# Adaptive average pooling: partition p owns block p/8 + 16 (p mod 8) of the rows in place of block p

## The chip, the cores and the metric

The kernel runs on one core of one Trainium2 chip. The metric is the time of one execution on the device in microseconds (us); lower is better. Before the change the median of three runs is 333.54 us (333.31 to 333.57).

## The reference

The input x has 32 batches of 256 channels of 4096 float32 values. The output has 256 values for each batch and channel: value i is the mean of the 16 neighbouring inputs from 16 i to 16 i + 15.

```
for i in range(output_size):
    start = int(i * length / output_size)
    end = int((i + 1) * length / output_size)
    result[:, :, i] = np.mean(x[:, :, start:end], axis=-1)
```

Batches and channels are alike for this, so the kernel sees 8192 independent rows of 4096 values (16 KiB) that become rows of 256 values (1 KiB). The input is 134.2 MB, the output 8.4 MB.

## The kernel before

The 8192 rows are worked through in 16 tiles of 512 rows: 128 partitions by R = 4 rows. The first 15 tiles come from the first 7680 rows. They are cut into 128 blocks of 60 neighbouring rows (960 KiB of input, 60 KiB of output), and partition p owns block p. In tile t each partition loads rows 4t to 4t+3 of its block, one contiguous run of 64 KiB, so that a load is 128 runs (8.4 MB). The sixteenth tile takes the last 512 rows, four neighbouring rows to a partition (x_last, o_last).

The pattern of a load has two sides. On the DRAM side x_many (line 46) is [partition][60 x 4096 values], from which line 69 cuts the 16384 values of tile t. On the SBUF side the tile xin is [128 partitions][16384 values].

In the loop (lines 62 to 88) each tile goes through the same steps:
- Line 70: SP issues the load of the tile into xin. The pool inpool (line 53) has two buffers, so the load of tile t+2 waits until the work on tile t is done.
- Line 73: POOL (GpSimd) takes the second half of the tile's 1024 windows and adds their upper 8 values to their lower 8, in place.
- Line 78: DVE (VectorE) sums the 16 values of each window of the first half, at the same time.
- Line 81: DVE sums the 8 values that POOL left of each window of the second half.
- Line 84: ACT (ScalarE) multiplies the 1024 sums by 1/16, in place.

The results of the 15 tiles stay in SBUF in res_many, 60 KiB for each partition, and leave in one store of 7.86 MB into o_many (line 47, issued by line 72 through store, line 58). SP issues it after the load of the last tile, once the ACT of tile 14 is done. The results of the last tile (res_last) leave in two stores at the end (line 90): 120 partitions, then the other 8.

All transfers are issued by SP, on one queue, in program order. Tile's scheduler places the waits of loads and compute; the three stores are counted on a semaphore of their own (line 60), on which SP waits at the end (line 95).

Of the kernel before, what the change touches and what calls it, by code (L numbers as in the profile page):

```python
# [1 line left out]

# [4 lines left out]


@with_exitstack
def kernel(  # L10
    ctx: ExitStack,
    tc: tile.TileContext,
    x: bass.AP,
    output_size: int,
    out: bass.AP,
):

    nc = tc.nc
    F32 = mybir.dt.float32
    X = mybir.AxisListType.X

    batch, channels, length = x.shape
    ob, oc, olen = out.shape
    assert ob == batch and oc == channels and olen == output_size
    assert length % output_size == 0
    window = length // output_size  # L30
    hw = window // 2
    inv_w = 1.0 / float(window)

    P = nc.NUM_PARTITIONS
    R = 4
    rows = batch * channels
    assert rows % (P * R) == 0
    ntiles = rows // (P * R)
    many = (ntiles - 1) * R
    cells = R * output_size  # L40
    m = cells // 2
    cols = R * length

    xr = x.rearrange("b c l -> (b c) l")
    orow = out.rearrange("b c o -> (b c) o")
    x_many = xr[0 : P * many, :].rearrange("(p r) l -> p (r l)", p=P, r=many)
    o_many = orow[0 : P * many, :].rearrange("(p r) o -> p (r o)", p=P, r=many)
    x_last = xr[P * many :, :].rearrange("(p r) l -> p (r l)", p=P, r=R)
    o_last = orow[P * many :, :].rearrange("(p r) o -> p (r o)", p=P, r=R)

    res_many = nc.alloc_sbuf_tensor("res_many", [P, (ntiles - 1) * cells], F32, align_bytes=256)
    res_last = nc.alloc_sbuf_tensor("res_last", [P, cells], F32, align_bytes=256)
    inpool = ctx.enter_context(tc.tile_pool(name="inpool", bufs=2))

    stored = nc.alloc_semaphore("stored")

    def store(out, in_):
        ins = nc.sync.dma_start(out=out, in_=in_)
        tc.no_tile_sem_insts.add(ins.ins.name)
        ins.then_inc(stored, 16)  # L60

    for t in range(ntiles):
        last = t == ntiles - 1
        xin = inpool.tile([P, cells, window], F32, name="xin")
        if last:
            res, base, src = res_last, 0, x_last
        else:
            res, base = res_many, t * cells
            src = x_many[:, t * cols : (t + 1) * cols]
        nc.sync.dma_start(out=xin.rearrange("p o w -> p (o w)"), in_=src)  # L70
        if last:
            store(o_many, res_many[:, :])
        nc.gpsimd.tensor_add(  # L73
            out=xin[:, m:cells, 0:hw],
            in0=xin[:, m:cells, 0:hw],
            in1=xin[:, m:cells, hw:window],
        )
        nc.vector.reduce_sum(  # L78
            out=res[:, base : base + m], in_=xin[:, 0:m, :], axis=X
        )  # L80
        nc.vector.reduce_sum(  # L81
            out=res[:, base + m : base + cells], in_=xin[:, m:cells, 0:hw], axis=X
        )
        nc.scalar.mul(  # L84
            out=res[:, base : base + cells],
            in_=res[:, base : base + cells],
            mul=inv_w,
        )
    for lo, hi in ((0, 120), (120, P)):
        store(o_last[lo:hi, :], res_last[lo:hi, :])  # L90

    ctx.pop_all().close()
    tc.close()
    tc.compile()  # L94
    nc.sync.wait_ge(stored, 48)
    nc.sync.sem_clear(stored)


# [1 line left out]
_INS = ['x', 'output_size']  # L100
_OUTS = [((32, 256, 256), 'float32')]

_NUMBERS = {'output_size': 256}


# [26 lines left out]
```

## Time and profile before

| what | us |
|---|---|
| median of 3 runs | 333.54 (333.31 to 333.57) |
| the profiled execution, its own time | 333.37 |
| its span, from the first instruction to the last | 332.1 |
| first load lands (first reduction starts) | 22.72 |
| last load lands (last L78 starts) | 312.86 |
| large store issued | 307.67 |
| two small stores issued | 327.26 |
| L78 on DVE, one instruction | 8.69 |
| L73 on POOL, one instruction | 8.72 |
| L81 on DVE, one instruction | 4.42 |
| L84 on ACT, one instruction | 1.06 |
| median from a load's issue to its landing | 25.3 |

The page gives for each engine its busy time and its share of the span. DMA engines are no such engine: the core's 16 DMA engines are shown together, by the packets of each queue (number, MB, and the time that the packets took as a share of 16 engines' span), and by rows of 40 slices with the mean busy share in tenths and the GB/s moved. The bytes of a packet are counted where it starts, so that slices shorter than a packet jump up and down. There is one clock value for TensorE, which this kernel doesn't use. A load's time to landing includes the time that it stands behind the load ahead of it in the queue.

### The profile page before, as it was taken

The page shows a single profiled execution, that of the slowest core. Times are in us where ns is not written, and L with a number is a line of the kernel's source. Part 1 is how long each engine was busy: PE and PEld are TensorE (multiplying, and loading weights), DVE is VectorE, ACT ScalarE, POOL GpSimd, SP SyncE. Part 2 cuts the span into 40 slices and gives each one's busy share as a digit, 9 for nine tenths or more (in the row PEclk, how much of TensorE's full clock was granted, in tenths as well). Part 3 has the DMA queues.
Part 4 walks back from the last instruction along what each step waited for, and adds up shares of the span by engine and source line. Part 5 has one row for each costly group of instructions (what it writes and reads, how often), then busy time and mean ns, then how long its engine had stood idle before and what let it go on. Part 6 is the DMA issues. An engine that isn't in the chain of part 4 may idle for free.

```text
span 332.1 us, 160 instructions
## 1 busy us (share of the span) xinstructions
DVE 209.7 (63%) x32; ACT 18.2 (5%) x17; POOL 139.7 (42%) x20
## 2 busy tenths in 40 slices
DVE  0029396692939669293966939295693929569392
ACT  1000101001010100101010010101000010100001
POOL 0027091542709164270916427090643709063270
DMA  9898999989899998989899998989999898989997
GB/s 379 379 505 379 474 411 426 458 379 505 379 489 395 450 434 379 505 379 505 379 474 411 395 489 379 505 379 489 395 450 434 379 505 379 505 379 474 395 466 307
DMA packets 2599, 142.61 MB, mean 429 GB/s; under 512 B 295, under 2 KB 295, under 8 KB 423
## 3 DMA queue, kind: packets, MB, share of 16 engines
q1 hardware_dynamic: 2599, 142.61, 99.4%
HBM read 134.22 MB, written 8.39 MB: 429 GB/s over the span
## 4 chain that ended last, share of the span: by engine, by line
DMA 66%; POOL 18%; DVE 11%; POOLq 3%; issue 0%; ACT 0%; SPq 0%
DMA xin<-in_x_dram 66%; POOL xin L73 18%; DVE res_many L81 9%; POOLq L94 3%; DVE res_last L81 1%; ACT res_last L84 0%; SPq L70 0%; POOLq L73 0%
## 5 line engine op out<-in xcount | busy, mean ns | idle before, releaser
L73 POOL TENSOR_TENSOR xin<-xin 128x4096 f32<-128x4096 f32 x16 | 139.5, 8719 | 181.7 <-DMA xin<-in_x_dram 181.7
L78 DVE TENSOR_REDUCE res_many<-xin 128x512 f32<-128x8192 f32 x15 | 130.3, 8686 | 107.4 <-DMA xin<-in_x_dram 107.4
L81 DVE TENSOR_REDUCE res_many<-xin 128x512 f32<-128x4096 f32 x15 | 66.3, 4420 | 2.5 <-POOL xin L73 2.3
L84 ACT ACTIVATE res_many<-res_many 128x1024 f32<-128x1024 f32 x15 | 15.9, 1057 | 289.8 <-DVE res_many L81 289.8
L78 DVE TENSOR_REDUCE res_last<-xin 128x512 f32<-128x8192 f32 x1 | 8.7, 8686 | 6.3 <-DMA xin<-in_x_dram 6.3
L81 DVE TENSOR_REDUCE res_last<-xin 128x512 f32<-128x4096 f32 x1 | 4.4, 4420 | 0.2 <-POOL xin L73 0.2
L84 ACT ACTIVATE res_last<-res_last 128x1024 f32<-128x1024 f32 x1 | 1.1, 1057 | 18.5 <-DVE res_last L81 18.5
L84 ACT ACT_TABLE_LOAD x1 | 1.3, 1283 | 0.7 <-PEq L113 0.7
L113 POOL MEMSET const-float32-0.0<- 128x1 f32 x1 | 0.1, 99 | 0.2 <-issue 0.2
L113 POOL MEMSET const-bfloat16-1.0<- 128x1 bf16 x1 | 0.1, 103 | 0.0
L113 POOL MEMSET const-uint8-127<- 128x1 uint8 x1 | 0.1, 103 | 0.0
L113 POOL MEMSET const-float32-1.0<- 128x1 f32 x1 | 0.1, 99 | 0.0
## 6 DMA issues: line engine op xcount, KB each, us to landing
out_dram<-res_many SPq DMA_DIRECT2D x1, 7680.0 KB
out_dram<-res_last SPq DMA_DIRECT2D x1, 480.0 KB
xin<-in_x_dram SPq DMA_DIRECT2D x16, 25.3
out_dram<-res_last SPq DMA_DIRECT2D x1, 32.0 KB
```

The costliest lines, as they stand in the source:

```text
L73: nc.gpsimd.tensor_add(out=xin[:, m:cells, 0:hw], in0=xin[:, m:cells, 0:hw], in1=xin[:, m:cells, hw:window],)
L78: nc.vector.reduce_sum(out=res[:, base : base + m], in_=xin[:, 0:m, :], axis=X)
L81: nc.vector.reduce_sum(out=res[:, base + m : base + cells], in_=xin[:, m:cells, 0:hw], axis=X)
L84: nc.scalar.mul(out=res[:, base : base + cells], in_=res[:, base : base + cells], mul=inv_w,)
L94: tc.compile()
L113: nc = _bacc.Bacc("TRN2", target_bir_lowering=False, num_devices=1)
```

## The change

The 128 blocks of 60 rows are given to the partitions in another order. The DRAM sides of the 15 loads and of the large store get a dimension more: 16 (a) by 8 (b), where partition 8a + b owns block 16b + a. Partition 0 owns block 0, partition 1 block 16, partition 7 block 112, partition 8 block 1, and so on. Partitions that follow each other within a group of eight are 16 blocks (15 MiB of input) apart in DRAM; partitions that are eight apart own neighbouring blocks. The SBUF sides are as before, as are the last tile, all compute instructions and the order of issue. Load and store use the same order, so each result goes to its own row.

```diff
     xr = x.rearrange("b c l -> (b c) l")
     orow = out.rearrange("b c o -> (b c) o")
-    x_many = xr[0 : P * many, :].rearrange("(p r) l -> p (r l)", p=P, r=many)
-    o_many = orow[0 : P * many, :].rearrange("(p r) o -> p (r o)", p=P, r=many)
+    A = 16
+    B = P // A
+    x_many = xr[0 : P * many, :].rearrange("(b a r) l -> a b (r l)", a=A, b=B, r=many)
+    o_many = orow[0 : P * many, :].rearrange("(b a r) o -> a b (r o)", a=A, b=B, r=many)
     x_last = xr[P * many :, :].rearrange("(p r) l -> p (r l)", p=P, r=R)
     o_last = orow[P * many :, :].rearrange("(p r) o -> p (r o)", p=P, r=R)
...
             res, base = res_many, t * cells
-            src = x_many[:, t * cols : (t + 1) * cols]
+            src = x_many[:, :, t * cols : (t + 1) * cols]
         nc.sync.dma_start(out=xin.rearrange("p o w -> p (o w)"), in_=src)
         if last:
             store(o_many, res_many[:, :])
```

## The prediction

> **What bounds the kernel now.** I read the sum of the page first (busy time by engine, then the DMA queue), then the chain that ended last, then a table of stretches that I cut where the first packets start (1.73, from the 40 slices of the first 3 us) and where reductions start, then the timeline around one issue. The page says which resource is full:
>
> ```profile
> DVE 209.7 (63%) x32; ACT 18.2 (5%) x17; POOL 139.7 (42%) x20
> ...
> q1 hardware_dynamic: 2599, 142.61, 99.4%
> HBM read 134.22 MB, written 8.39 MB: 429 GB/s over the span
> ...
> DMA 66%; POOL 18%; DVE 11%; POOLq 3%; issue 0%; ACT 0%; SPq 0%
> ```
>
> No engine is busy for more than 63% of the span, while the packets of the one DMA queue fill 99.4% of what 16 DMA engines have. The chain names POOL and DVE too (18% and 11%), but that is the buffer's turn: a load is issued when its buffer is free and then queues behind the load before it. The table of stretches says what a load costs in the steady state (columns: stretch, its length, busy time of DVE, ACT and POOL, granted clock, share of the 16 DMA engines, GB/s):
>
> ```profile
> 1.73:22.72 20.99, 0.00 (x1) 0.29 (x1) 0.00 (x0) 1.00 1.07 450
> ...
> 80.74:273.96 193.22, 131.06 (x20) 10.57 (x10) 87.19 (x10) 1.00 1.00 434
> ...
> 293.27:312.86 19.59, 13.11 (x2) 1.06 (x1) 8.72 (x1) 1.00 0.99 425
> ```
>
> A packet counts where it starts, which gives the first stretch a share above 1: it holds starts of the second load. The middle row spans ten loads: 193.22 / 10 = 19.32 us a load, at a DMA share of 1.00. Per load DVE works 13.1 us and POOL 8.7 us; both then wait. A load moves 128 x 64 KiB = 8.39 MB, and 8.39 MB / 19.32 us is the 434 GB/s of the row, 27.1 GB/s for each of 16 engines. The timeline shows how far ahead of need a load is issued:
>
> ```profile
> 94.05 0.33 SPq L70 DMA_DIRECT2D xin<-in_x_dram  x1
> 94.05 1.06 ACT L84 ACTIVATE res_many<-res_many 128x1024 f32<-128x1024 f32 x1 [18.33 <-DVE res_many L81]
> 100.07 8.69 DVE L78 TENSOR_REDUCE res_many<-xin 128x512 f32<-128x8192 f32 x1 [6.05 <-DMA xin<-in_x_dram]
> ```
>
> The load is issued at 94.05, the one ahead of it lands at 100.07: 6.0 us of spare time for the issue. So time moves only if the rate of the 16 DMA engines moves, or the first load's start, or the tail.
>
> **The change, part by part.** No instruction is added or removed. The same 15 loads (L70) and the one large store (L58, 7.86 MB) keep their bytes, their number of contiguous runs (128 runs of 64 KiB a load, 128 of 60 KiB in the store) and their SBUF side. Two things differ, both on the DRAM side.
>
> *Which rows a partition reads.* The blocks stay 60 rows = 960 KiB apart, in another order. The trace shows 434 GB/s with one order and no other. Below: nothing, the runs are as long as before. Above: no row shows a load slowed by DRAM placement, and the nearest one is the first load, 20.99 us in place of 19.32, which carries the cold start. If every one of the 14 other changed loads ran like that it would be 14 x 1.67 = 23.4 us. I take 0: the steady rows are flat at 434 to 435 GB/s over addresses that move on with every load.
>
> *The shape of the DRAM side.* It was [128][run], it is [16][8][run], while the SBUF side stays [128][run]. If the 16 DMA engines share a transfer by its outermost dimension, then each now gets one of the 16 outer entries, and so eight neighbouring partitions (8a to 8a+7), in that order. Which engine serves which partition isn't in the trace. If the old split gave each engine a way into SBUF of its own, and the new one lets two engines meet on one way while another way stands empty, a load takes up to twice its time.
>
> Bounds for one load: nothing is gained below, since the share is already 1.00; above, 2 x 19.32 = 38.64 us, +19.32. For the 15 changed loads: 0 to 15 x 19.32 = +289.8 us. The sixteenth load (x_last) keeps its shape. For the large store: at 434 GB/s it takes 7.86 / 434 = 18.1 us, so 0 to +18.1.
>
> Which end? For the direction out of SBUF there is a near row. The tail's 480 KB store has 120 partitions, which 16 doesn't divide, so it can't have the split of a 128-partition transfer. It fills most of the last microsecond of traffic:
>
> ```profile
> DMA  7839977339997079999087994843994000000000
> GB/s 328 328 164 655 655 328 328 164 164 819 492 492 328 0 328 655 492 492 492 0 328 328 655 655 164 328 164 164 492 656 164 0 0 0 0 0 0 0 0 0
> DMA packets 95, 0.30 MB, mean 295 GB/s; under 512 B 23, under 2 KB 23, under 8 KB 95
> ```
>
> This is the stretch 330.7 to 331.7, in 40 slices. Traffic fills 31 of them: 295 x 40 / 31 = 381 GB/s with packets of 4 KiB, no sign of a halving (217). So I put the large store at +0 and keep +18.1 for the range. For the direction into SBUF no row shows any split but the old one; the rows are at 434, the two ends are 0 and +289.8. I take the upper end, and that is a choice: the present rate is exactly flat at full share, which is how 16 separate ways look, and the change pairs engines up with nothing in it that sets them apart.
>
> [...]
>
> *Issue.* A three-dimensional pattern may cost SP more than the 0.33 us of a load's issue. The 6.0 us between issue and the landing of the load ahead hide that; with loads twice as long the spare time is longer still. Without that cover each extra microsecond would cost 15.
>
> *Waits and the compute engines.* The change adds no wait. DVE and POOL work on the same tiles; they wait 19 us longer per load if the loads double. Nothing queues behind that except the ACT scaling and the next issue, which has the whole of the longer load ahead of it. The tail is as before: last load, 13.2 us of POOL and DVE beside the large store, ACT, two small stores.
>
> **The sum.** The profiled execution: span 332.1, time 333.37, so 1.3 us lie around the span, and the median of the runs shown, 333.54, is 0.17 above it. 333.37 + 289.8 (15 loads) + 0 (store) = 623.2. [...] The 16 first packets start from 1.73 to 2.85, within about a microsecond of each other, by the same 40 slices; with 0.1 us for the pair that is closest together, 15 x 0.2 = 3 us come off. With the 0.17: 620.
>
> **Rivals.**
> *A, two engines meet all the way (forecast).* 620; 600 with a lead of 0.8 us (15 x 1.6 = 24 off), 641 with no lead and a doubled store. For it: a share of exactly 1.00 and a regrouping that pairs engines. Against it: the 120-partition store. If only 8 engines took part the loads would double as well, and the DMA share of the loads would show 0.5.
> *B, the pairs draw apart.* If one engine of a pair gets more of the shared way, its lead grows, and a lead of half a load (9.66 us) ends the meeting. [...] Anything from 340 to 600. A DRAM order that is dearer (up to +23.4) falls into its lower end, 334.2 to 357.
> *C, nothing meets (the other side: not slower).* The ways into SBUF have room for two engines, as the ways out seem to have in the 120-partition store. Then the share of 1.00 is the engines' own limit, every load stays at 19.32 us, and the time is 333.5. It decides if the loads still run at 434 GB/s.
> *D, faster.* C, and the new order also takes away the cold start of the first load (20.99 - 19.32 = 1.7 us) and the slower last one (19.59 - 19.32 = 0.3 us): at most 2.0 us, 331.5 to 332.8. The rest is bytes at full share, so nothing larger can be gained.
>
> **How the numbers follow.** A 0.54, B 0.27 (0.04 of it below 345), C 0.14, D 0.05. The time is A's, 620. The range reaches from 345 to 645: all of A and B but its lowest part, 0.77, about what is asked; going on to C would take in 0.95 and a stretch in which little lies. A measurement of this kernel tells about 0.2% from no change. Faster by over 0.2%: D, 0.05. Within: C, 0.14. Slower: A and B, 0.81.
>
> **What the changed kernel's profile would show.** Under A: the starts of L78's reductions 38 us apart in place of 19.32, stretches of loads near 220 GB/s with a packet share that stays near 1.00 (packets last longer, all 16 engines hold one), the same 2599 packets, DVE near 34% of the span, and the last load (the unchanged shape) back at about 19.6 us. The large store back at 18 us puts the doubling on the way in alone; 36 us puts it on both. Under B the distance between reductions shrinks from load to load. Under C the page is the same to the tenth. A packet count other than 2599 would mean that runs were cut, and my price for the shape would be wrong from the start; so would loads that double with a share of 0.5.

## The result, and the profile after

The changed kernel takes 669.53 us (median of three runs, 668.88 to 669.72) against 333.54 us before: 2.007 times as long, 95% interval 2.004 to 2.009. The direction was as forecast, the time lies 24.5 us above the upper end of the range (645). The profiled execution took 668.88 us with a span of 667.6. Where runs of one kernel further down lie more than 1.5% apart (pairs_apart_2, pitch_64_rows), the faster ones are the ones to compare.

The page of the changed kernel, the same lines as before the change (the lines of the code are two further down now: L72 is the load, L75 POOL, L80 and L83 DVE, L86 ACT, L60 the stores):

```profile
DVE 209.7 (31%) x32; ACT 18.2 (3%) x17; POOL 139.7 (21%) x20
...
q1 hardware_dynamic: 2599, 142.61, 99.7%
HBM read 134.22 MB, written 8.39 MB: 214 GB/s over the span
```

The engines are busy for the same 209.7, 18.2 and 139.7 us. The queue has the same 2599 packets and the same 142.61 MB, and its share of the 16 DMA engines is 99.7%, as full as before. Yet the rate is 214 GB/s in place of 429. A full share says only that every DMA engine holds a packet at all times, not that the packets move at full speed: by their records the median packet of 64 KiB takes 5.12 us in place of 2.42.

The table of stretches of the changed kernel, cut at the starts of the reductions (stretch, length, busy time of DVE, ACT and POOL, granted clock, DMA share, GB/s):

```profile
84.43:570.56 486.13, 157.27 (x25) 12.67 (x12) 104.61 (x12) 1.00 1.00 207
611.30:630.37 19.07, 13.11 (x3) 1.06 (x1) 8.72 (x1) 1.00 1.01 436
630.37:667.60 37.23, 13.10 (x2) 1.06 (x1) 8.72 (x1) 1.00 0.92 199
```

The first row is twelve loads of the new shape: 486.13 / 12 = 40.51 us a load in place of 19.32, at 207 GB/s. The second row is the last load, which kept its shape: 19.07 us, 436 GB/s, on the same queue with the 16 engines just as full (share 1.01). The third row is the tail with the large store: 37.23 us, where the kernel before had

```profile
312.86:332.06 19.20, 13.11 (x2) 1.06 (x1) 8.72 (x1) 1.00 0.89 386
```

The difference of the two spans, 667.6 - 332.1 = 335.5, closes over these pieces. The last reduction of the 15 changed tiles starts at 611.30 in place of 293.27, +318.0 (15 x 21.2). The last load gives back 19.59 - 19.07 = 0.5, and the tail costs 37.23 - 19.20 = +18.0.

The issue of a load costs SP more with the three-dimensional pattern, 0.54 us in place of 0.33 in the steady state, and lies under 27 us of spare time, as these two lines of the changed kernel's timeline show:

```profile
178.77 0.54 SPq L72 DMA_DIRECT2D xin<-in_x_dram  x1
...
205.97 8.69 DVE L80 TENSOR_REDUCE res_many<-xin 128x512 f32<-128x8192 f32 x1 [27.23 <-DMA xin<-in_x_dram]
```

### The profile page after: what moved, and what is told of

It is laid out like the page before. It is cut to its first block, busy times and chain, and to the rows that moved or that the text cites. A ratio compares the mean times of both kernels' runs of the same rounds, so it can differ in the third digit from the quotient of the medians.

```text
span 667.6 us, 160 instructions
## 1 busy us (share of the span) xinstructions
DVE 209.7 (31%) x32; ACT 18.2 (3%) x17; POOL 139.7 (21%) x20
## 2 busy tenths in 40 slices
DMA packets 2599, 142.61 MB, mean 214 GB/s; under 512 B 295, under 2 KB 295, under 8 KB 423
## 3 DMA queue, kind: packets, MB, share of 16 engines
q1 hardware_dynamic: 2599, 142.61, 99.7%
## 4 chain that ended last, share of the span: by engine, by line
another core or an unknown queue 62%; POOL 18%; DMA 13%; POOLq 1%; DVE 1%; issue 0%; ACT 0%
POOL xin L75 18%; DMA xin<-in_x_dram 13%; POOLq L96 1%; DVE res_last L83 1%; DVE res_many L83 1%; ACT res_last L86 0%; POOLq L75 0%
## 5 line engine op out<-in xcount | busy, mean ns | idle before, releaser
L80 DVE TENSOR_REDUCE res_many<-xin 128x512 f32<-128x8192 f32 x15 | 130.3, 8686 | 425.5 <-DMA xin<-in_x_dram 425.5
L75 POOL TENSOR_TENSOR xin<-xin 128x4096 f32<-128x4096 f32 x16 | 139.5, 8718 | 499.3 <-DMA xin<-in_x_dram 499.3
L83 DVE TENSOR_REDUCE res_many<-xin 128x512 f32<-128x4096 f32 x15 | 66.3, 4420 | 2.5 <-POOL xin L75 2.3
L86 ACT ACTIVATE res_many<-res_many 128x1024 f32<-128x1024 f32 x15 | 15.8, 1056 | 607.8 <-DVE res_many L83 607.8
L80 DVE TENSOR_REDUCE res_last<-xin 128x512 f32<-128x8192 f32 x1 | 8.7, 8686 | 5.8 <-DMA xin<-in_x_dram 5.8
L83 DVE TENSOR_REDUCE res_last<-xin 128x512 f32<-128x4096 f32 x1 | 4.4, 4420 | 0.2 <-POOL xin L75 0.2
L86 ACT ACTIVATE res_last<-res_last 128x1024 f32<-128x1024 f32 x1 | 1.1, 1056 | 18.0 <-DVE res_last L83 18.0
```

The costliest lines, as they stand in the source:

```text
L75: nc.gpsimd.tensor_add(out=xin[:, m:cells, 0:hw], in0=xin[:, m:cells, 0:hw], in1=xin[:, m:cells, hw:window],)
L80: nc.vector.reduce_sum(out=res[:, base : base + m], in_=xin[:, 0:m, :], axis=X)
L83: nc.vector.reduce_sum(out=res[:, base + m : base + cells], in_=xin[:, m:cells, 0:hw], axis=X)
L86: nc.scalar.mul(out=res[:, base : base + cells], in_=res[:, base : base + cells], mul=inv_w,)
```

## The experiments

Theory 1 is that of the forecast: the shape of the DRAM side. It supposes that with an outer dimension of 16 each DMA engine gets eight neighbouring partitions, and that two engines are then always on the same way into or out of SBUF; no trace shows which engine serves which partition. Theory 2, the rival, is the order of the blocks in DRAM: engines that read adjacent blocks, or blocks 15 MiB apart, are slow together. The change made both edits at once. Beside each group of runs the kernel before was timed again; its medians are 333.33 to 333.58 us, and the ratios below are to these.

### The shape without the order, and the order with it: loads_old_order, loads_only

The first keeps the neighbourhood of the old order. The 4 rows between groups are there so that the two dimensions can't be merged into one.

```diff
-    x_many = xr[0 : P * many, :].rearrange("(b a r) l -> a b (r l)", a=A, b=B, r=many)
+    x_many = xr[0 : A * 484, :].rearrange("(a s) l -> a s l", a=A, s=484)[:, 0 : B * many, :]
+    x_many = x_many.rearrange("a (b r) l -> a b (r l)", b=B, r=many)
-    o_many = orow[0 : P * many, :].rearrange("(b a r) o -> a b (r o)", a=A, b=B, r=many)
+    o_many = orow[0 : P * many, :].rearrange("(p r) o -> p (r o)", p=P, r=many)
```

> The 15 loads keep the [16][8] shape, but partition 8a + b reads a block that lies next to its old one (block 8a + b, moved on by 4a rows so that the two dimensions don't merge into one); the large store has its old shape and old places. Left out and changed: results of blocks a > 0 are those of rows 4a further on. Theory 1, the shape (each engine gets eight neighbouring partitions, and two engines meet on one way into SBUF): the loads stay at 40.5 us as in the changed kernel, 15 x 21.2 = 318 over the kernel before, so about 651 us. Theory 2, the order of the blocks in DRAM: the old order is back, 19.32 us a load, about 333.5 us.

Measured: 651.04 us (ratio 1.952, 1.946 to 1.958). The second run has the last edit alone, the store's:

> Changed kernel, but the large store has its old one-dimensional shape and places. Changed: the results of a partition go to the place of block p. Both theories: the loads at 40.5 us, the store back from 36.4 to 18.1 us, 669.5 - 18.3 = 651 us. What it tells apart is whether the store's share of the loss is its own (651) or the tail of the loads (669).

Measured: 651.33 us (ratio 1.953, 1.947 to 1.958). The two agree to 0.3 us although their loads read in quite different orders. The stretch of twelve loads, first in loads_old_order (84.99 to 570.92), then in loads_only (84.55 to 570.20):

```profile
84.99:570.92 485.93, 157.27 (x25) 12.67 (x12) 104.61 (x12) 1.00 1.00 207
```

```profile
84.55:570.20 485.65, 157.28 (x25) 12.67 (x12) 104.60 (x12) 1.00 1.00 207
```

40.49 and 40.47 us a load. The shape alone carries the whole loss of the loads; the new order of the blocks costs nothing that these runs can tell. That two engines meet on SBUF's side is not yet shown by this: it only shows that where in DRAM they read makes no difference here.

### The store alone: store_only, store_old_order

store_only has the old x_many and the new o_many.

> Kernel before, but the large store has the new shape and order. Changed: results go to other places. If the ways out of SBUF are shared in the same manner as the ways in, the store takes 36.4 us in place of 18.1: 333.5 + 18.3 = 352 us. If the store was slow in the changed kernel only because it follows the loads, 333.5 us.

Measured: 351.06 us (ratio 1.053, 1.050 to 1.056), +17.5 us. store_old_order adds the same trick with 4 rows between groups on the store's side:

> store_only with the [16][8] shape, but in the old neighbourhood: partition 8a + b stores to the place of block 8a + b moved on by 4a rows (of the last tile's rows 64 are not stored, 16 partitions). Theory 1, the shape: 351 us as in store_only. Theory 2, the order of the places in DRAM makes the store slow: 333.5 us.

Measured: 352.10 us (ratio 1.056, 1.053 to 1.059). So the store's doubling is its own and the shape's too. By the records of its 128 packets of 60 KiB, the median one took 4.72 us in store_only and 2.27 us in the kernel before.

### How many engines, how many ways: eight_engines

```diff
-    A = 16
+    A = 8
```

> Changed kernel with the outer dimension 8 and the inner 16 (partition 16a + b owns block 8b + a) for loads and large store. [...] Theory 1 with meetings between two engines: 8 engines with 16 packets each, each packet 5.07 us as in the changed kernel, 81.1 us a load: 2.2 + 15 x 81.1 + 19.8 + 16 x 4.79 + 1.5 = about 1317 us, DMA share about 0.5. If nothing met and only the number of engines counted: packets of 2.418 us, 38.7 us a load, 2.2 + 15 x 38.7 + 19.8 + 16 x 2.267 + 1.5 = about 640 us, share 0.5. If the outer dimension doesn't set the engines: 669 us, share 1.0.

Measured: 1296.44 us (ratio 3.887, 3.835 to 3.938). The page of this kernel:

```profile
DMA packets 2471, 142.61 MB, mean 109 GB/s; under 512 B 167, under 2 KB 167, under 8 KB 295
## 3 DMA queue, kind: packets, MB, share of 16 engines
q1 hardware_dynamic: 2471, 142.61, 51.4%
```

A share of 51.4% in place of 99.7%: with the outer dimension of 8, half of the engines' time holds no packet. There are 128 packets fewer than the 2599 of the changed kernel, all among those under 512 B (167 in place of 295), eight for each of the 16 changed transfers. Both fit eight engines in place of 16. And in the time that holds a packet the data move at half speed as well: 107 GB/s at a share of 0.50 over the stretch of four loads, 13.4 GB/s for each of eight engines in place of 27.1,

```profile
163.98:482.11 318.13, 52.43 (x9) 4.22 (x4) 34.87 (x4) 1.00 0.50 107
```

79.5 us a load, a quarter of the old rate. Were the number of engines all that counts, it would be 38.7 us and 640 us in all. One factor of two is in the share; the other fits engines that meet, as theory 1 expected with about 1317 us, but this run shows neither that they meet nor on what.

### Setting the pairs apart: two_rows, two_rows_pairs_apart, two_rows_pairs_together

Which engines meet, if any do, is in no trace; that it is engines e and e + 4 is an assumption of these runs. If those two meet because they walk through the same ways in step, a head start of half a load for one of them should end it, although the shape stays as it is. For this the tiles are halved, so that four loads can be under way.

```diff
-    R = 4
+    R = 2
-    inpool = ctx.enter_context(tc.tile_pool(name="inpool", bufs=2))
+    inpool = ctx.enter_context(tc.tile_pool(name="inpool", bufs=4))
```

> Changed kernel with tiles of 2 rows a partition (runs of 32 KiB) and 4 buffers: 31 loads of the new shape and one of the old. It is the control for the two runs with a head start. Theory 1: a load takes half of 40.5 us, 31 x 20.25 us, and the total stays near 669 us, since engines that meet still meet all the way.

Measured: 671.38 us (ratio 2.014, 2.006 to 2.021). The two runs with small loads ahead, which assume that a transfer on n partitions goes to the first n engines, add, with 12 and 4 partitions or with 8,

```diff
+    for n, first in ((12, 0), (12, 1), (12, 2), (12, 3), (4, 4), (4, 5), (4, 6), (4, 7)):
+        nc.sync.dma_start(
+            out=res_many[first : first + 9 * (n - 1) + 1 : 9, 0:cols],
+            in_=xr[0 : n * R, :].rearrange("(p r) l -> p (r l)", p=n, r=R),
+        )
```

> As two_rows, with 8 small loads of 32 KiB a partition ahead of the first (into res_many, which is written over later): four on 12 partitions and four on 4 partitions. If a transfer on n partitions is dealt to the first n engines, engines 0 to 3 get 8 packets, 4 to 11 get 4, 12 to 15 get none, so that each engine e is four packets, half a load, apart from engine e + 4. Theory 1 with pairs e and e + 4 on one way: the meetings end and stay ended, a load takes about 9.7 to 11 us, the store partly doubled: 333.5 + 10 (small loads) + 5 to 45 = 350 to 390 us. Theory 2 (DRAM order) or other pairs: no gain, 669 + 10 = about 680 us.

> As two_rows, with 8 small loads on 8 partitions each, the same 64 packets of 32 KiB in all: engines 0 to 7 start 8 packets behind engines 8 to 15, and the engines e and e + 4 stay level. Theory 1 with pairs e and e + 4: no gain, 669 + 10 = about 680 us. If any unevenness of the engines ended the meetings: near 350 to 400 us, as in two_rows_pairs_apart.

Measured: 670.10 us (ratio 2.010, 2.006 to 2.014) and 687.90 us (ratio 2.063, 2.053 to 2.073). Neither came near 350 to 390: this experiment failed to show what it was made for. The timeline of SP in two_rows_pairs_apart shows that the head start was small (start, duration, issue):

```profile
0.73 5.79 SPq L60 DMA_DIRECT2D res_many<-in_x_dram  x8
6.57 3.98 SPq L78 DMA_DIRECT2D xin<-in_x_dram  x4
```

Eight small loads hold SP for 5.79 us, and the first large load is issued at 6.57. Four packets of 1.21 us (their length at full speed, by the records) can be over by then, so by the assumed deal engines 4 to 11 may have had no delay left and only engines 0 to 3 started late. The records don't show even these apart: of the 3888 packets of 32 KiB that start between 12 and 600 us, none takes less than 2.16 us. So either the lead was lost at once, or engines that meet slow the others too. This run can't tell which.

### The same with longer small loads: pairs_apart_2, pairs_together_2

In place of the eight small loads of 32 KiB a partition:

```diff
+    w = 15360
+    for n, first in ((12, 0), (12, 1), (12, 2), (12, 3), (4, 4), (4, 5)):
+        nc.sync.dma_start(
+            out=res_many[first : first + 9 * (n - 1) + 1 : 9, 0:w],
+            in_=xr[0 : n * 4, :].rearrange("(p r) l -> p (r l)", p=n, r=4)[:, 0:w],
+        )
```

> [...] Here the small loads are fewer and longer: four of 60 KiB on 12 partitions, two on 4 partitions, so that both groups of pairs start about 4.5 us apart (half a load is 4.84). Theory 1 with pairs e and e + 4: loads of 9.7 to 11 us, 333.5 + 14 (the last engines' start) + up to 30 = 345 to 380 us. If the pairs are others, or no lead lasts: 671 + 14 = about 685 us.

> Control for pairs_apart_2: seven small loads of 60 KiB on 8 partitions, the same 56 packets, so that engines 0 to 7 start 16 us behind engines 8 to 15 and e and e + 4 stay level. Theory 1 with pairs e and e + 4: no gain, 671 + 16 = about 687 us. If any unevenness among the engines ended the meetings: near pairs_apart_2.

Measured: pairs_apart_2 takes 444.37 and 463.62 us in two runs (the profile is of the second), pairs_together_2 702.54 us (699.23 to 705.85; ratio 2.106, 2.083 to 2.130), 15 us more than expected. The same 56 packets, on 12 and 4 partitions in place of 8, are worth 235 us or more. A table of stretches of pairs_apart_2 (17 loads):

```profile
61.09:263.67 202.58, 114.00 (x34) 10.69 (x17) 75.65 (x17) 1.00 1.00 352
```

and of pairs_together_2:

```profile
60.00:640.00 580.00, 199.25 (x60) 18.87 (x30) 131.56 (x30) 1.00 1.00 212
```

202.58 / 17 = 11.92 us a load of 4.19 MB at 352 GB/s, against 19.8 us a load at 212 GB/s: with the shape, the order and the bytes unchanged, most of the loss goes with the small loads that by the assumed deal set e and e + 4 apart, and none of it with those that set engines 0 to 7 apart from 8 to 15. Half of the old 19.32, 9.66 us, is what no meeting at all would give.

Two limits of this pair of runs. It rests on the assumption that a transfer on n partitions goes to the first n engines, which the records (without engine numbers) can't confirm. And it sets groups apart, 0 to 3 from 4 to 7 and 8 to 11 from 12 to 15: that inside a group e goes with e + 4 is inferred, not shown.

The forecast of 345 to 380 us was missed, and only in part because the gain didn't last:

```profile
37.60:377.68 340.08, 187.76 (x56) 17.61 (x28) 124.56 (x28) 1.00 1.01 350
377.68:412.65 34.97, 13.41 (x4) 1.26 (x2) 8.90 (x2) 1.00 0.83 224
422.00:462.30 40.30, 6.71 (x2) 0.63 (x1) 4.46 (x1) 1.00 0.86 183
```

The first row is 28 loads of 12.15 us, where 9.7 to 11 were forecast: by theory 1 the pairs were never fully apart, and this alone is 32 us or more. The second is two loads of 15.4 and 19.6 us, in which the gain goes. The third is the tail with the large store, whose packets take 4.91 us in the median. The GB/s row of the page shows the same, in 40 slices of 11.6 us:

```profile
GB/s 267 229 340 360 352 363 337 357 349 349 349 346 337 360 360 360 357 357 337 357 354 357 332 349 335 352 346 332 352 352 335 352 335 255 224 117 187 176 220 155
```

Up to slice 33, about 380 us, the rate stays near 350; then it falls to 255 and 224. Nothing in the kernel keeps the pairs apart. What made the gain end there wasn't tried.

One thing in the records doesn't fit two engines that slow only each other. The small packets of 60 KiB that start before the first packets of a large load (7.7 us of the span in pairs_apart_2, 8.0 in pairs_together_2) take 2.28 to 3.34 us. Those that start between 9.8 and 13 us, 12 in the one run and 8 in the other, all take 4.56 us or more. By the assumed deal the large load is then on engines 12 to 15 in the one run and 8 to 15 in the other, and the small packets' engines 0 to 7 should meet none of these. Either a meeting slows engines that have no part in it, or the deal of the small loads is not the assumed one; no run here settles it.

### Why the tail's small store showed no loss: store_4k_new, store_4k_old, store_15k

The forecast put the large store at no cost on the strength of the tail's store of 120 partitions and 4 KiB each. store_4k_new cuts the large store of store_only into the same length of run:

```diff
-            store(o_many, res_many[:, :])
+            for i in range(ntiles - 1):
+                store(o_many[:, :, i * cells : (i + 1) * cells], res_many[:, i * cells : (i + 1) * cells])
-    nc.sync.wait_ge(stored, 48)
+    nc.sync.wait_ge(stored, 16 * (ntiles + 1))
```

> store_only with the large store cut into 15 stores of 4 KiB a partition, each in the new shape. It asks why the 120-partition store of the tail, which moves 4 KiB a partition, ran without a sign of meeting. If runs of 4 KiB don't meet: 18 us for the store, about 334 us. If they do: 36 us, about 352 us, and the tail's store was only too short to show it.

> Control for store_4k_new: the same 15 stores in the old shape, nothing can meet. Both theories: about 334 us; more would be the price of 15 issues.

Measured: 334.44 us (ratio 1.004, 1.002 to 1.006) in the new shape, 334.22 us (ratio 1.002, 1.001 to 1.003) in the old. All 1920 packets of the store in the new shape took 159 ns by their records, like the tail's. A middle length, four stores of 15 KiB:

```diff
+            w = (ntiles - 1) * cells // 4
+            for i in range(4):
+                store(o_many[:, :, i * w : (i + 1) * w], res_many[:, i * w : (i + 1) * w])
```

> store_only with the large store cut into 4 stores of 15 KiB a partition in the new shape, between store_4k_new (334.4 us, no packet above 159 ns) and store_only (351.1 us). If a run must be long for two engines to meet: between the two, some packets of 0.57 us and some of up to 1.2 us. If it is the number of stores that parts the engines: nearer to 334.

Measured: 340.73 us (ratio 1.022, 1.019 to 1.025), +7.3 us, 0.4 of the way from none to all. Its 512 packets take 0.573 us at best, 0.578 us in the median and 1.12 us at the ninth tenth. So out of SBUF, with this shape, the loss grows with the length of the runs: none at 4 KiB, 7 us at 15, 17.5 at 60. Cutting the store shortens the runs and each transfer alike, and these runs don't tell the two apart.

### The same on the way in: loads_4k, loads_4k_old

loads_only with each of the 15 loads cut into 16:

```diff
+            w = cols // 16
+            for i in range(16):
+                nc.sync.dma_start(out=flat[:, i * w : (i + 1) * w], in_=src[:, :, i * w : (i + 1) * w])
```

> loads_only with each of the 15 loads cut into 16 loads of 4 KiB a partition in the new shape (240 issues; at most 8 are under way). Changed as in loads_only: results of a partition go to the place of block p. If runs of 4 KiB don't meet on the way in, as they didn't on the way out: the control's time, 333.5 to 360 us. If only the way out has room for short runs: about 651 us or more.

> Control for loads_4k: the same 240 loads of 4 KiB a partition in the old shape. Nothing can meet: 333.5 us and whatever 240 issues with 8 under way cost, 0 to 25 us. It prices the cutting.

Measured: 553.65 us (ratio 1.660, 1.644 to 1.677) in the new shape, 343.86 us (ratio 1.031, 1.028 to 1.034) in the old. Neither expectation of loads_4k holds: cutting into short runs and short transfers helps on the way in, but the shape still costs 553.65 - 343.86 = 210 us where runs of 64 KiB cost 318. The stretch of thirteen loads of loads_4k:

```profile
55.36:500.00 444.64, 175.47 (x27) 13.73 (x13) 113.34 (x13) 1.00 1.03 249
```

249 GB/s, with a median packet of 285 ns against 159 ns in the control. About eight of the 240 loads are under way at a time: 16.8 us in the median from issue to landing, at 444.64 / 208 = 2.14 us each. Sixteen loads in place of one also cost 10 us with the old shape.

### Does the order in DRAM ever matter: pitch_64_rows

The kernel before, with its one-dimensional shape, but 64 rows to a partition (60 for the 15 tiles, 4 for the last):

```diff
-    x_many = xr[0 : P * many, :].rearrange("(p r) l -> p (r l)", p=P, r=many)
+    x64 = xr.rearrange("(p s) l -> p s l", p=P, s=R * ntiles)
+    x_many = x64[:, 0:many, :].rearrange("p r l -> p (r l)")
```

and the same for x_last and both outputs.

> Kernel before with the old one-dimensional shape, but another order of rows in DRAM: partition p owns rows 64p to 64p + 63 (60 in the 15 tiles, 4 in the last), so that blocks are 1 MiB apart in place of 960 KiB. Theory 1: the order of rows doesn't matter, 333.5 us. Theory 2: a power of two between the partitions is at least as bad an order as the changed kernel's, and the time moves by many per cent. [...]

Measured: 351.60, 356.35, 359.80 and 359.99 us in four runs. These runs spread too far for an interval, but all four lie over 17 us above every run of the kernel before. The page of the run of 356.35 us:

```profile
DMA packets 2599, 142.61 MB, mean 402 GB/s; under 512 B 295, under 2 KB 295, under 8 KB 423
## 3 DMA queue, kind: packets, MB, share of 16 engines
q1 hardware_dynamic: 2599, 142.61, 98.5%
```

An order with blocks 1 MiB apart does cost 5% or more (351.60 and 356.35 against 333.33), so theory 2 names something real. It is not what this change ran into, as loads_old_order and loads_only show.

## Why the prediction was wrong

**The bound** was read rightly: the rate of the DMA engines set the time before and sets it after (434 and 207 GB/s, both at a share of 1.00), and all other engines do the same work in the same time.

**The mechanism** was right as far as it is shown. Of rival A, engines that meet because of the shape, the shape is shown for the loads: it alone gives 651 us. Small loads that by the assumed deal set the engines apart by groups of four give most of the loads' loss back (11.92 us a load in place of 19.8). That engines meet, and on a way into SBUF, is inferred (two orders in DRAM gave the same loss), that each gets eight neighbouring partitions and that e meets e + 4 is assumed and shown by no run, and the small packets of pairs_together_2 say that more than two engines may be slowed by it. The end of the range to take was a choice, as the forecast said: no row ahead of it showed the new split. The share of exactly 1.00, which it counted for A, tells nothing of that: the share is 99.7% at half the rate too.

**The step that failed is the sum: two of its terms were mis-sized**, and one deduction was wrong.

- "I put the large store at +0": it cost 18.0 us in the changed kernel and 17.5 alone. This is the term that failed by reasoning. The tail's store ran at 381 GB/s and was taken as a sign that the ways out have room for two engines. It has runs of 4 KiB, the large store has 60 KiB, and store_4k_new shows that the length, of the run or of the transfer, was the difference. The small store, at 159 ns a packet, shows no loss; for the large one the +18.1 that the range kept was the right term.
- "15 x 19.32 = +289.8" took twice the old time as the upper end for a load. A load costs 40.51 us, 2.10 times the old one. 15 x (40.51 - 38.64) = 28 us lie above what I had called a bound. If the engines do meet in eight pairs, a pair moves 207 / 8 = 25.9 GB/s, less than the 27.1 (434 / 16) that one engine moved before: then they don't just halve each other.
- "3 us come off" for a lead of 0.1 us within a pair, twice the lead from each load: no run shows this term, neither the lead nor what it takes off, nor the 24 us by which the 600 was reached in the same way. The runs showed 15 loads at 40.51 us, above twice the old 19.32, and no gain.

620 + 18 (store) + 28 (loads above twice) + 3 (lead) = 669, the measured time. With the store alone put right the sum would be 638, inside the range; it is the loads' term that leaves it. The range ended at 645 because it rested on the same bound of twice the time. Twice the time is the end only if two that share one lose nothing between them; 2.10 was measured.

**Issue and waits** were as said: SP's longer issue is hidden, the last load is back at 19.07 us, no wait was added, and the packet count is 2599. DVE is at 31% of the span (34% expected) and the share of the queue stays full, which the forecast had named as the sign of engines that meet and not of engines that are missing.

**The rivals.** B (pairs draw apart) gets nothing: 40.5 us from the third load to the last but one. In pairs_apart_2 the time of a load does change along the run: from 11.8 us to 13.6, back to 12.0 and at the end to 19.6, by theory 1 from apart to together. C and D are refuted by the loads' rate.

## What to carry to other kernels

A reordering that looks like a change of addresses alone can halve the rate, because it changes the shape of the pattern: here an outer dimension of 16 on the DRAM side gave 207 GB/s in place of 434, and one of 8 gave 107. Keep 128 outermost on both sides of such a load, as in the 434 GB/s here, or time the new shape first. A DMA share of 99% does not mean that the engines run at full speed (99.4% at 429 GB/s here, 99.7% at 214); divide the GB/s by the engines and compare with a stretch known to be good. A row taken as evidence for another transfer must match it in run length and direction: 4 KiB runs out of SBUF (159 ns a packet) said nothing about 60 KiB runs out of it (4.72 us a packet in place of 2.27), nor about 4 KiB runs into it (285 ns).

## What the runs showed of the hardware beyond the forecast

- Out of SBUF, the new shape runs at full speed with runs of 4 KiB (159 ns a packet, all 1920), loses part of it with 15 KiB (+7.3 us) and half of it with 60 KiB (+17.5 us on a store of 18.1). Into SBUF, runs of 4 KiB lose less than runs of 64 KiB (249 against 207 GB/s), but two thirds of the loss stays (210 of 318 us). What does this was not settled.
- An outer dimension of 8 gives a share of 51.4%, as eight working engines would, and a quarter of the rate (107 against 434 GB/s).
- A load on 4 to 12 partitions takes SP 0.58 to 0.94 us to issue (median 0.66, two_rows_pairs_apart), one of the old shape on 128 partitions 0.33 us.
- Blocks 1 MiB apart in DRAM cost 18 to 23 us against blocks 960 KiB apart, with the same shape and runs (351.60 and 356.35 us). The loads carry it: in the profiled run the last one lands at 335.47 in place of 312.86, and the tail takes 19.5 us in place of 19.2.
